# Gate and up projections of a SwiGLU layer by seven half products instead of eight, on one Trainium2 core

## The chip, the cores and the metric

The kernel runs on one core of one Trainium2 chip. The metric is the device time of one execution in microseconds (us), the median of three runs. TensorE (PE in the profile) multiplies, and loads the stationary operand of each product in a row of its own (PEld). VectorE (DVE) and ScalarE (ACT) work on tiles in SBUF and PSUM, GpSimd (POOL) adds squares, and SyncE (SP) issues the DMAs.

## The reference

One decoder layer on 512 tokens of width 1024: a SwiGLU feed-forward sub-layer, a mixer (a spatial-gating half and an attention half), cross-attention into 256 memory rows, and a second SwiGLU sub-layer. The change concerns the two feed-forward sub-layers; their hidden width is 2816.

```
def rmsnorm(t, g):
    tf = t.astype(F32)
    y = tf * lax.rsqrt(jnp.mean(tf * tf, axis=-1, keepdims=True) + NORM_EPS)
    return (y * g.astype(F32)).astype(t.dtype)
def swiglu(h, w_gate, w_up, w_down):
    return (jax.nn.silu(h @ w_gate) * (h @ w_up)) @ w_down
...
h = rmsnorm(x, ffn1_norm[l])
x = x + 0.5 * swiglu(h, ffn1_w_gate[l], ffn1_w_up[l], ffn1_w_down[l])
```

## The kernel before

Features lie on partitions and tokens on the free axis, so the residual stream is eight tiles X[0..7] of 128 x 512. Every fp32 operand is split in two rounded parts: ScalarE copies it to a high part (L103), and VectorE subtracts that from the source for a low part (L104). One fp32 product is then three matmuls (`mm3`, L127 to L129): high by high, low by high, high by low.

A feed-forward sub-layer (`ffn`) has 22 hidden tiles of 128 features, called f. For each f a gate weight tile and an up weight tile of 128 x 1024 come in, one DMA of 512 KB each, into a raw tile (`wraw`); `load_weight` splits it into `whi` and `wlo`. Each of the three names has three buffers. A weight tile takes 8 x 3 matmuls of 512 columns against the eight split tiles of x times gain (hH, hL). The row factor R (one over the root mean square) is not in these operands: `evacuate` multiplies both results by it (L243, L247), applies Silu, multiplies, and splits the product into hidH and hidL. After eleven hidden tiles a down projection adds to X: for each of eight output columns d two weight loads, 33 matmuls, and one VectorE addition (L230). So the sub-layer has two such chunks. In the last chunk of the second sub-layer the down projection runs in two halves of 256 tokens, each followed by the final normalisation and its output DMAs.

The work is written in program order; a scheduler then sets the order on each engine and in each DMA queue, and it is fixed from there on: an engine, and SP's queue of DMA issues, takes its rows one after the other, and a row that waits holds what stands behind it. The pool `hp` has 40 buffers of 128 x 512 for operands of all kinds, `pacc` and `paux` four PSUM banks each.

## Time and profile before

| what | before |
|---|---|
| median of three runs | 1129.87 us (1128.18 to 1129.97) |
| the profiled execution's own time | 1129.09 us |
| its span, first to last instruction | 1127.3 us |
| PE busy | 1110.1 us, 98% of the span |
| DVE busy | 590.9 us, 52% |
| ACT busy | 425.0 us, 38% |
| POOL busy | 74.3 us, 7% |

Busy time adds up the durations of an engine's rows, overlap counted once. Matmuls are pipelined, so a row of 390 ns does not mean that the next starts 390 ns later; what counts is the distance between starts. An idle time before a group of rows names what ended it. A window's row gives, per engine, the busy time and the number of instructions, then the granted TensorE clock (1.00 is full), the share of the DMA engines, and GB/s.

### The profile page before, as it was taken

To read this page: it belongs to the slowest core of one execution; us is meant where nothing else is said; L and a number is where in the kernel's file an instruction comes from. 1 tells how busy PE (TensorE), PEld (TensorE's weight loads), DVE (VectorE), ACT (ScalarE), POOL (GpSimd) and SP (SyncE) were. 2 spreads that over 40 slices of the span, in tenths; PEclk is the share of its full clock that TensorE was granted. 3 is DMA by queue.
4 is the path that set the end of the run, shared out by engine and by line. 5 is a ranking of instruction groups with operands and counts; after the bars stand their busy time and mean duration, and the time that the engine had idled before them with its cause. 6 is when DMAs were issued, how large, how long until landed. Compare 5 with 4: busy or idle time off the path is not lost. (4 is left out here: it accounts for less than half of the span.)

```text
span 1127.3 us, 13958 instructions
## 1 busy us (share of the span) xinstructions
PE 1110.1 (98%) x5472; PEld 934.7 (83%) x5472; DVE 590.9 (52%) x1027; ACT 425.0 (38%) x672; POOL 74.3 (7%) x98
## 2 busy tenths in 40 slices
PE   9999999999999999999989999999999999999996
PEld 7788888888888888888868988878888888888996
DVE  4544533444444447679796555455444334445542
ACT  6333312233233434568665344333332222333421
POOL 2000100000002200011121000120000000000011
PEclk9999999999999999999999999999999999999998
DMA  6322334222233423110136421222222333223511
GB/s 220 113 94 89 115 89 126 105 94 94 72 92 109 149 90 108 38 48 29 57 118 203 147 75 57 72 97 90 98 93 66 103 113 111 95 94 115 155 64 38
DMA packets 39698, 110.79 MB, mean 98 GB/s; under 512 B 4432, under 2 KB 9296, under 8 KB 39632
## 3 DMA queue, kind: packets, MB, share of 16 engines
q1 hardware_dynamic: 39632, 109.89, 30.3%
q8 instruction: 43, 0.70, 0.2%
q14 instruction: 23, 0.19, 0.1%
HBM read 107.78 MB, written 2.10 MB: 97 GB/s over the span
## 5 line engine op out<-in xcount | busy, mean ns | idle before, releaser
L103 ACT ACTIVATE whi<-wraw 128x1024 fp32r<-128x1024 f32 (+2 forms) x213 | 202.8, 953 | 513.9 <-PE acc L128 298.6
L104 DVE TENSOR_TENSOR wlo<-wraw,whi 128x1024 fp32r<-128x1024 f32 (+2 forms) x213 | 237.0, 1115 | 163.0 <-ACT whi L103 162.7
L127 PE MATMUL acc<-hH,whi 128*128 128x512 f32 x768 | 301.0, 392 | 0.6 <-ACT hH L202 0.6
L128 PE MATMUL acc<-hL,whi 128*128 128x512 f32 x768 | 299.4, 390 | 0.8 <-DVE hL L203 0.8
L129 PE MATMUL acc<-hH,wlo 128*128 128x512 f32 x768 | 299.4, 390 | 0.5 <-DVE wlo L104 0.5
L128 PEld LDWEIGHTS acc<-hL,whi 128*128 128x128 f32 x768 | 144.3, 188 | 31.5 <-DVE hL L203 1.5
L127 PEld LDWEIGHTS acc<-hH,whi 128*128 128x128 f32 x768 | 144.3, 188 | 31.4 <-ACT hH L202 1.0
L129 PEld LDWEIGHTS acc<-hH,wlo 128*128 128x128 f32 x768 | 144.3, 188 | 30.7 <-DVE wlo L104 1.0
L127 PE MATMUL acc<-hidH,whi 128*128 128x512 f32 (+1 forms) x308 | 115.6, 375 | 0.0
L129 PE MATMUL acc<-hidH,wlo 128*128 128x512 f32 (+1 forms) x308 | 115.3, 374 | 0.0
L128 PE MATMUL acc<-hidL,whi 128*128 128x512 f32 (+1 forms) x308 | 115.3, 374 | 0.0
L170 POOL TENSOR_TENSOR sq<-sq 128x512 f32<-128x512 f32 (+1 forms) x39 | 49.2, 1260 | 775.5 <-ACT sq L178 775.1
L247 DVE TENSOR_TENSOR u<-acc,R 128x512 f32<-128x512 f32 x44 | 30.4, 690 | 121.6 <-PE acc L129 121.6
L243 DVE TENSOR_TENSOR gp<-acc,R 128x512 f32<-128x512 f32 x44 | 30.4, 691 | 85.4 <-PE acc L129 81.7
L129 PEld LDWEIGHTS acc<-hidH,wlo 128*128 128x128 f32 x308 | 58.1, 189 | 10.3
L128 PEld LDWEIGHTS acc<-hidL,whi 128*128 128x128 f32 x308 | 58.1, 188 | 10.3
L127 PEld LDWEIGHTS acc<-hidH,whi 128*128 128x128 f32 x308 | 58.1, 189 | 10.2
L127 PE MATMUL acc<-whi,hH 128*128 128x512 f32 x160 | 62.5, 391 | 0.0
L129 PE MATMUL acc<-whi,hL 128*128 128x512 f32 x160 | 62.4, 390 | 0.0
L230 DVE SCALAR_TENSOR_TENSOR x<-acc,x 128x512 f32<-128x512 f32 (+1 forms) x40 | 23.3, 584 | 74.6 <-PE acc L129 74.6
L128 PE MATMUL acc<-wlo,hH 128*128 128x512 f32 x160 | 62.3, 390 | 0.0
L178 ACT ACTIVATE sq<-x 128x512 f32<-128x512 f32 (+1 forms) x48 | 26.1, 551 | 41.5 <-DVE x L230 38.9
(213 smaller groups left out, 1488.1 us busy)
## 6 DMA issues: line engine op xcount, KB each, us to landing
wraw<-up SPq DMA_DIRECT2D x44, 512.0 KB, 3.5
wraw<-gate SPq DMA_DIRECT2D x43, 512.0 KB, 3.5
wraw<-down SPq DMA_DIRECT2D x28, 384.0 KB, 3.1
wraw<-w_in SPq DMA_DIRECT2D x20, 512.0 KB, 3.5
wraw<-down SPq DMA_DIRECT2D x28, 320.0 KB, 2.9
wraw<-w_out SPq DMA_DIRECT2D x16, 256.0 KB, 2.7
wraw<-wv SPq DMA_DIRECT2D x8, 512.0 KB, 3.5
wraw<-wk SPq DMA_DIRECT2D x8, 512.0 KB, 4.2
```

Of the source, the lines that this page charges most:

```text
L103: ins = nc.scalar.activation(hi, src, AF.Copy)
L104: nc.vector.tensor_sub(lo, src, f32(hi))
L127: nc.tensor.matmul(ps, lhsT=aH, rhs=bH, start=start, stop=False)
L128: nc.tensor.matmul(ps, lhsT=aH, rhs=bL, start=False, stop=False)
L129: nc.tensor.matmul(ps, lhsT=aL, rhs=bH, start=False, stop=stop)
L170: nc.gpsimd.tensor_add(self.parts[0], self.parts[0], sq)
L178: nc.scalar.activation(sq, src, AF.Square)
L230: nc.vector.scalar_tensor_tensor(X[d][:, tok], acc, 0.5, X[d][:, tok], op0=ALU.mult, op1=ALU.add)
L243: nc.vector.tensor_mul(gp, ps[0], R)
L247: nc.vector.tensor_mul(u, ps[1], R)
```

## The change

The first two pairs of hidden tiles (f = 0 to 3) of a sub-layer stay as they were, and are now a chunk of their own. The other nine pairs go in three chunks of three pairs. For such a pair the gate product, and the up product likewise, is seen as a 2 x 2 block product: two weight tiles (rows r1 and r2 of the source), two halves of the inner dimension (k0 and k1), two halves of the tokens (LO and HI). It is formed by seven products of half the inner dimension and 256 tokens, in place of eight. The products are numbered 1 to 7 in the code; each is 4 x 3 matmuls of 256 columns. They accumulate in turns in few PSUM banks, and ScalarE copies what is needed of a stage before the next product adds to it (p1, p5, v); VectorE combines the rest.

The right operands (B11, B2, T13, T24) hold x times gain times R and differences of such tiles. `operands(k)`, called four times while f = 2 and 3 are worked on, makes them. With R in the operands, nothing is multiplied by R behind the product.

The left operands of a pair need, for each source, the two plain halves of r1 (in the raw tile `a1`, named wraw), a quarter `a22` (named wr), and four sums (ws1 to ws4). The quarter `q` (named wq) starts as r2's first half; an accumulating DMA from POOL's queue adds r2's second half; it is split as ws1; VectorE adds r1's first half; it is split as ws2; a second accumulating DMA adds r1's second half, and it is split as ws4. A third accumulating DMA adds r2's first half into the raw tile `a1` itself, which is split as ws3. So each source of a pair has three accumulating DMAs of 256 KB, and seven splits of 128 x 512 where there were two of 128 x 1024. The quarters and their splits live in `hp`, as the hidden tiles now do.

The down projections take four chunks (4, 6, 6 and 6 hidden tiles), each with one weight load per column; two columns are begun before the last two hidden tiles are there. `mem_rows`, a side computation on the memory rows, moves its two small later steps into the mixer.

```diff
-with tc.tile_pool(name="ffn", bufs=2) as fp:
+with tc.tile_pool(name="spad", bufs=1) as spad, \
+        tc.tile_pool(name="sp", bufs=1) as sp, \
+        tc.tile_pool(name="ffn", bufs=1) as fp:
+    nc.vector.memset(spad.tile([P, SHIFT], F32, name="spad")[:, 0:1], 0.0)
     R = None
-    def down_tile(d, w, hid, tok, jj, acc=None, js=range(CF)):
+    B11, B2 = ([], []), ([], [])
+    T13, T24 = ([], []), ([], [])
+    def operands(k):
+        x = []
+        for d in (k, k + KH):
+            t = hp.tile([P, S], F32, name="xg", tag="h")
+            nc.vector.scalar_tensor_tensor(t, X[d], gcol(norm.off, d), R,
+                                           op0=ALU.mult, op1=ALU.mult)
+            x.append(t)
+        a, b = x
+        t13 = hp.tile([P, S], F32, name="t13", tag="h")
+        nc.vector.tensor_sub(t13[:, LO], a[:, LO], a[:, HI])
+        nc.vector.tensor_sub(t13[:, HI], b[:, HI], a[:, HI])
+        t24 = hp.tile([P, S], F32, name="t24", tag="h")
+        nc.vector.scalar_tensor_tensor(t24[:, LO], b[:, HI], -1.0, t13[:, LO],
+                                       op0=ALU.mult, op1=ALU.subtract)
+        nc.vector.scalar_tensor_tensor(t24[:, HI], t24[:, LO], -1.0, b[:, LO],
+                                       op0=ALU.mult, op1=ALU.subtract)
+        for n, pair, src in (("b11", B11, a[:, LO]), ("b2", B2, b),
+                             ("t13", T13, t13), ("t24", T24, t24)):
+            for i, hl in enumerate("hl"):
+                pair[i].append(sp.tile([P, src.shape[-1]], F32R, name=f"{n}{hl}{k}"))
+            split(pair[0][k], pair[1][k], src)
+    def c_tile(name):
+        return fp.tile([P, S], F32, name=name, tag="c", bufs=5)
+    def half_tile(name):
+        return fp.tile([P, S // 2], F32, name=name, tag="half", bufs=5)
...
+    def down_tile(d, w, hid, tok, acc=None, js=None, cut=((0, 8),)):
+        n = len(hid[0])
         if acc is None:
             acc = acc_tile()[:, tok]
...
-    def evacuate(ps, hid):
-        gp = fp.tile([P, S], F32, name="gp", tag="gp")
-        nc.vector.tensor_mul(gp, ps[0], R)
-        s = fp.tile([P, S], F32, name="s", tag="s")
-        nc.scalar.activation(s, gp, AF.Silu)
-        u = fp.tile([P, S], F32, name="u", tag="u")
-        nc.vector.tensor_mul(u, ps[1], R)
-        nc.vector.tensor_mul(u, s, u)
-        hH = fp.tile([P, S], F32R, name="hidH", tag="hidH", bufs=12)
-        hL = fp.tile([P, S], F32R, name="hidL", tag="hidL", bufs=12)
+    def hidden(u, hid):
+        hH, hL = h_tile("hidH"), h_tile("hidL")
         split(hH, hL, u)
         hid[0].append(hH)
         hid[1].append(hL)
+    def evacuate(ps, hid):
+        gp = c_tile("gp")
+        nc.vector.tensor_mul(gp, ps[0], R)
+        nc.scalar.activation(gp, gp, AF.Silu)
+        u = c_tile("u")
+        nc.vector.tensor_mul(u, ps[1], R)
+        nc.vector.tensor_mul(u, gp, u)
+        hidden(u, hid)
+    def plain(f, src):
+        if f == 0 and src is gate and first is not None:
+            w = first()
+        else:
+            w = load_weight(src[f], [KD, P])
+        acc = acc_tile()
+        for k in range(KD):
+            mm3(acc, w, h, (slice(None), k), k, k == 0, k == KD - 1)
+        return acc
+    def quarter(name, dtype=F32R):
+        return hp.tile([P, KH, P], dtype, name=name, tag="h")
+    def strassen_weights(src, j, wa):
+        k0, k1 = slice(0, KH), slice(KH, KD)
+        r1, r2 = src[2 * j], src[2 * j + 1]
+        a1 = wp.tile([P, KD, P], F32, name="wraw", tag="wraw")
+        q, a22 = quarter("wq", F32), quarter("wr", F32)
+        nc.sync.dma_start(q, r2[:, k0])
+        nc.sync.dma_start(a1, r1)
+        last["dma"] = nc.sync.dma_start(a22, r2[:, k1])
+        nc.gpsimd.dma_start(q, r2[:, k1], accum_op=ALU.add)
+        def parts(raw, name):
+            w = quarter(name + "h"), quarter(name + "l")
+            split(w[0], w[1], raw)
+            return w
+        w = {1: wa[0], 2: wa[1]}
+        split(*w[1], a1[:, k0])
+        w[5] = parts(q, "ws1")
+        nc.vector.tensor_add(q, q, a1[:, k0])
+        w[6] = parts(q, "ws2")
+        nc.gpsimd.dma_start(a1[:, k0], r2[:, k0], accum_op=ALU.add)
+        nc.gpsimd.dma_start(q, r1[:, k1], accum_op=ALU.add)
+        split(*w[2], a1[:, k1])
+        w[7] = parts(a1[:, k0], "ws3")
+        w[3] = parts(q, "ws4")
+        w[4] = parts(a22, "wa22")
+        return w
+    def strassen(j, hid):
+        right = {1: (B11, LO), 2: (B2, LO), 3: (B2, HI), 4: (T24, HI),
+                 5: (T13, LO), 6: (T24, LO), 7: (T13, HI)}
+        wa = [[wp.tile([P, KD, P], F32R, name=n, tag=n) for n in ("whi", "wlo")]
+              for _ in range(2)]
+        W = [strassen_weights(src, j, [tuple(x[:, s * KH:(s + 1) * KH] for x in pair)
+                                       for pair in wa])
+             for s, src in enumerate((gate, up))]
+        z = [acc_tile()[:, HI] for _ in range(2)]
+        b1, b5 = [None] * 2, [None] * 2
...
+        def product(ps, i, s, start):
+            b, tok = right[i]
+            wH, wL = W[s][i]
+            for k in range(KH):
+                bH, bL = b[0][k][:, tok], b[1][k][:, tok]
+                for n, (x, y) in enumerate(((wH, bH), (wH, bL), (wL, bH))):
+                    nc.tensor.matmul(ps, lhsT=x[:, k], rhs=y,
+                                     start=start and k == 0 and n == 0,
+                                     stop=k == KH - 1 and n == 2,
+                                     skip_group_check=True)
+        def copied(ps, name):
+            t = half_tile(name)
+            nc.scalar.activation(t, ps, AF.Copy)
+            return t
+        for s in range(2):
+            product(z[s], 1, s, True)
+            p1[s] = copied(z[s], "p1")
+        for s in range(2):
+            b5[s] = aux_tile()[:, HI]
+            product(b5[s], 5, s, True)
+            p5[s] = copied(b5[s], "p5")
+        for s in range(2):
+            product(z[s], 6, s, False)
+            v[s] = copied(z[s], "v")
+        for s in range(2):
+            b1[s] = aux_tile()[:, HI]
+            product(b1[s], 2, s, True)
+            nc.vector.tensor_add(c1[s][:, LO], b1[s], p1[s])
+        for s in range(2):
+            product(z[s], 7, s, False)
+            nc.vector.scalar_tensor_tensor(c2[s][:, HI], z[s], -1.0, p5[s],
+                                           op0=ALU.mult, op1=ALU.subtract)
+        for s in range(2):
+            product(b5[s], 3, s, False)
+            nc.vector.tensor_add(c1[s][:, HI], b5[s], v[s])
+        for s in range(2):
+            product(z[s], 4, s, False)
+        nc.scalar.activation(c1[0], c1[0], AF.Silu)
+        nc.scalar.activation(c2[0][:, HI], c2[0][:, HI], AF.Silu)
+        nc.scalar.activation(c2[0][:, LO], z[0], AF.Silu, scale=-1.0)
+        nc.vector.tensor_mul(c1[1], c1[0], c1[1])
+        hidden(c1[1], hid)
+        nc.vector.tensor_mul(c2[1][:, HI], c2[0][:, HI], c2[1][:, HI])
+        nc.vector.scalar_tensor_tensor(c2[1][:, LO], z[1], -1.0, c2[0][:, LO],
+                                       op0=ALU.mult, op1=ALU.mult)
+        hidden(c2[1], hid)
+    chunks = ((0, PLAIN),) + tuple((j, j + 3) for j in range(PLAIN, NF // 2, 3))
+    for c, (j0, j1) in enumerate(chunks):
         hid = ([], [])
+        for j in range(j0, j1):
+            if j >= PLAIN:
+                strassen(j, hid)
+                continue
+            for f in (2 * j, 2 * j + 1):
+                ps = [plain(f, gate)]
+                if R is not None and f > 1:
+                    operands(2 * f - 4)
+                if f == 1 and R is None:
+                    R = factor()
+                ps.append(plain(f, up))
+                pending.append(ps)
+                if first is None and f == 0:
+                    R = factor()
+                if R is not None:
+                    while pending:
+                        evacuate(pending.pop(0), hid)
+                if f > 1:
+                    operands(2 * f - 3)
+        f0, n = 2 * j0, 2 * (j1 - j0)
+        if c < len(chunks) - 1 or nxt is not None:
+            early = {}
+            for d in range(2):
+                w = [load_weight(down[d, :, f0:f0 + n, :], [n, P])]
+                early[d] = w, down_tile(d, w, hid, slice(0, S), None, range(n - 2))
+            for d in range(KD):
+                if d in early:
+                    w, acc = early[d]
+                    down_tile(d, w, hid, slice(0, S), acc, range(n - 2, n))
+                    w = [load_weight(down[d, :, f0:f0 + n, :], [n, P])]
+                    down_tile(d, w, hid, slice(0, S))
+                if c == len(chunks) - 1:
                     nxt.add(d)
-                elif between is not None:
-                    between(d)
+                    if between is not None:
+                        between(d)
             continue
...
-        thirds = ((0, 4), (4, 8), (8, CF))
+        cut = ((0, 4), (4, 6))
+        def weights(d):
+            if d not in kept:
+                raw = wp.tile([P, n, P], F32, name="wraw3", tag="wraw")
+                nc.sync.dma_start(raw, down[d, :, f0:f0 + n, :])
+                a, b, m = (h_tile("wk").rearrange("p (j m) -> p j m", m=P)
+                           for _ in range(3))
+                kept[d] = [(a, b), (m[:, 0:2], m[:, 2:4])]
+                for pair, (i0, i1) in zip(kept[d], cut):
+                    split(*pair, raw[:, i0:i1])
+            return kept[d]
...
             if t0 == 0:
-                for d in range(2):
-                    w, cut = weights(d, True)
-                    early[d] = down_tile(d, w, hid, tok, cut, None, range(CF - 1))
+                for d in range(3):
+                    early[d] = down_tile(d, weights(d), hid, tok, None, range(n - 2),
+                                         cut)
...
     z_block(norm, 0, gelu_to(U), lambda: col.append(norm.stats.column(D)))
+    mem_rows(2)
     z_block(norm, 1, gelu_to(V))
+    mem_rows(4)
...
 with tc.issue_after(last["dma"].ins):
     if d == 0:
         cs.append(rotary_tables(small))
-    mem_rows(d)
+        mem_rows(0)
...
-return np.ascontiguousarray(w.reshape(NCHUNK, CF, P, KD, P).transpose(0, 3, 2, 1, 4))
+return np.ascontiguousarray(w.reshape(NF, P, KD, P).transpose(2, 1, 0, 3))
```

What the scheduler makes of it is shown at three places of the second chunk of three pairs in the first sub-layer. The first place is SP's queue. Tiles are named with their numbers: 1836 and 1870 are the gate and up raw tiles of the chunk's first pair, 2118 and 2152 of its second, 2400 and 2434 of its third; wq and wr are the quarters of the tile numbered one or two lower. Before:

```order
L116 DMA wraw_687<-up1 128x1024
L116 DMA wraw_729<-gate1 128x1024
L116 DMA wraw_760<-up1 128x1024
L116 DMA wraw_802<-gate1 128x1024
L116 DMA wraw_833<-up1 128x1024
```

And with the change:

```order
L327 DMA wraw_2118<-gate1 128x1024
L327 DMA wraw_2152<-up1 128x1024
L326 DMA wq_1871<-up1 128x512
L328 DMA wr_1872<-up1 128x512
L327 DMA wraw_2400<-gate1 128x1024
L326 DMA wq_2119<-gate1 128x512
L328 DMA wr_2120<-gate1 128x512
L327 DMA wraw_2434<-up1 128x1024
L326 DMA wq_2153<-up1 128x512
L328 DMA wr_2154<-up1 128x512
L118 DMA wraw_2678<-down1 128x768
L118 DMA wraw_2697<-down1 128x768
```

The quarter of each source now stands behind the raw tile of a source three further on, which takes the buffer of the raw tile one source back. The second place is VectorE in the second pair, where whole-tile splits stood between evacuations before:

```order
L243 TENSOR_TENSOR gp_791<-acc_735,R_309 128x512
L104 TENSOR_TENSOR wlo_835<-wraw_833,whi_834 128x1024
L247 TENSOR_TENSOR u_795<-acc_766,R_309 128x512
L248 TENSOR_TENSOR u_795<-s_793,u_795 128x512
L104 TENSOR_TENSOR wlo_877<-wraw_875,whi_876 128x1024
L104 TENSOR_TENSOR hidL_799<-u_795,hidH_798 128x512
```

And with the change, the gate source (2118, 2119) and then the up source (2152, 2153):

```order
L106 TENSOR_TENSOR ws1l_2128<-wq_2119,ws1h_2127 128x512
L338 TENSOR_TENSOR wq_2119<-wq_2119,wraw_2118 128x512
L106 TENSOR_TENSOR ws2l_2133<-wq_2119,ws2h_2132 128x512
L106 TENSOR_TENSOR ws3l_2141<-wraw_2118,ws3h_2140 128x512
L106 TENSOR_TENSOR ws4l_2145<-wq_2119,ws4h_2144 128x512
L106 TENSOR_TENSOR wa22l_2149<-wr_2120,wa22h_2148 128x512
L106 TENSOR_TENSOR wlo_2397<-wraw_2434,whi_2396 128x512
L106 TENSOR_TENSOR wlo_2399<-wraw_2434,whi_2398 128x512
L106 TENSOR_TENSOR ws1l_2162<-wq_2153,ws1h_2161 128x512
L338 TENSOR_TENSOR wq_2153<-wq_2153,wraw_2152 128x512
L106 TENSOR_TENSOR ws2l_2167<-wq_2153,ws2h_2166 128x512
```

ws3 of the gate source is the last reader of raw tile 2118, whose buffer raw tile 2434 takes; the up source's ws1 stands behind. The third place is TensorE behind the second pair's gate products, with the change (before, each product was 24 matmuls of 512 columns into one accumulator, one weight tile after the other):

```order
L370 MATMUL acc_2469<-b11h3_602,whi_2396 128x256
L370 MATMUL acc_2469<-b11l3_603,whi_2396 128x256
L370 MATMUL acc_2469<-b11h3_602,wlo_2397 128x256
L370 MATMUL aux_2235<-t13h0_419,ws1h_2161 128x256
L370 MATMUL aux_2235<-t13l0_420,ws1h_2161 128x256
```

Product 1 of the third pair's up source (acc_2469) now stands ahead of product 5 of the second pair's up source (aux_2235), which in the code comes first.

More of the change, by code (lines that the diff above doesn't have):

```diff
@@ L41 @@
 SB = 6
+PLAIN = 2
 LINE = 512
 FILL = 56
+SHIFT = 112
 G_FFN1, G_MIX, G_CROSS, G_MEM, G_FFN2, G_FIN, G_OA, G_OB, G_BS = (
@@ L226, in down_tile @@
                                 mm3(acc, (wH, wL), hid, (slice(None), j - j0),
-                                    (j, slice(None), tok), j == 0, j == CF - 1)
-                    if CF - 1 not in js:
+                                    (j, slice(None), tok), j == 0, j == n - 1)
+                    if js is not None and n - 1 not in js:
                         return acc
@@ L286, in ffn @@
                                 nxt.add(d)
-                            elif between is not None:
-                                between(d)
+                                if between is not None:
+                                    between(d)
                         continue
-                    thirds = ((0, 4), (4, 8), (8, CF))
+                    cut = ((0, 4), (4, 6))
                     kept = {}
-                    def weights(d, keep):
-                        if d in kept:
-                            return kept[d], thirds
-                        if not keep:
-                            return [load_weight(down[c, d, :, j0:j1, :], [j1 - j0, P])
-                                    for j0, j1 in halves], halves
-                        kept[d] = []
-                        for j0, j1 in thirds:
-                            raw = wp.tile([P, j1 - j0, P], F32, name="wraw3", tag="wraw")
-                            nc.sync.dma_start(raw, down[c, d, :, j0:j1, :])
-                            pair = tuple(h_tile("wk")[:, :(j1 - j0) * P]
-                                         .rearrange("p (j m) -> p j m", m=P) for _ in range(2))
-                            split(*pair, raw)
-                            kept[d].append(pair)
-                        return kept[d], thirds
```

50 lines of the change are left out of this document (12 added, 38 removed).

## The prediction

> **What bounds the kernel now.** I read the page's busy times first, then its chain of waits, then busy time by window.
>
> ```profile
> PE 1110.1 (98%) x5472; PEld 934.7 (83%) x5472; DVE 590.9 (52%) x1027; ACT 425.0 (38%) x672; POOL 74.3 (7%) x98
> PE acc L128 11%; PE acc L129 11%; PE acc L127 11%; DVE o L330 0%; PE aux L153 0%; PE aux L186 0%; DVE rcolt L141 0%; DVE rcolt L142 0%; DVE rcoly L143 0%; DVE x L230 0%; ACT sq L178 0%; DVEq L889 0%; DVE dg L151 0%; DVE rcoly L136 0%; DVE rcolv L134 0%
> 32.00:273.00 241.00, 240.98 (x1063) 199.05 (x1062) 112.51 (x153) 72.31 (x94) 5.25 (x4) 1.00 0.31 99
> 1050.00:1107.00 57.00, 57.00 (x474) 56.87 (x473) 22.11 (x50) 14.26 (x26) 7.87 (x10) 1.00 0.28 86
> ```
>
> TensorE has no gap: the chain is matmuls, and in the feed-forward windows (columns: length, then PE, PEld, DVE, ACT, POOL, clock, DMA share, GB/s) it is busy throughout at full clock. The first window holds 512-column matmuls and gives 241.0 / 1063 = 0.2267 us from start to start; the second, the token-halved down projection, holds 256-column ones and gives 57.0 / 474 = 0.1203. VectorE has half its time free, DMA two thirds. So less matmul time shows in the span, as long as operands arrive in time.
>
> **What the change removes.** A pair cost 4 x 24 x 0.2267 = 21.8 us; now it is 2 x 7 x 12 = 168 matmuls at 0.1203 = 20.2. The saving is 1.55 us, not an eighth (2.7), since a 256-column matmul takes 53% of a 512-column one. Eighteen pairs give 27.9. In the last down projection five of eleven hidden tiles leave the halved form: 120 x (2 x 0.1203 - 0.2267) = 1.7. The tail behind the last matmul does not change.
>
> The Trainium skill ("TensorE: Matmul & The Clock Gate", section Back-to-back issue gap) has 262 and 518 cycles, 109 and 216 ns at 2.4 GHz. By these a pair would save 20.7 - 18.3 = 2.4 us; the windows' spacing decides, and gives 1.55.
>
> **What it adds on VectorE and ScalarE.**
>
> ```profile
> L104 DVE TENSOR_TENSOR wlo<-wraw,whi 128x512 fp32r<-128x512 f32 x18 | 12.1, 686 | 1.3 <-ACT whi L103 1.2
> L103 ACT ACTIVATE whi<-wraw 128x512 fp32r<-128x512 f32 x18 | 11.3, 628 | 5.5 <-PE acc L128 3.0 <-PE acc L129 1.9 <-DMA wraw<-gate 0.3
> L104 DVE TENSOR_TENSOR kL<-acc,kH 128x256 fp32r<-128x256 f32 x8 | 3.3, 418 | 0.0
> L466 DVE SCALAR_TENSOR_TENSOR vL<-acc,rcoly,vH 128x512 fp32r<-128x512 f32 x4 | 3.0, 749 | 1.7 <-ACT vH L465 1.7
> L666 DVE SCALAR_TENSOR_TENSOR mraw<-mraw,gains,R 128x256 f32<-128x256 f32 x8 | 3.7, 479 | 0.0
> L247 DVE TENSOR_TENSOR u<-acc,R 128x512 f32<-128x512 f32 x44 | 30.4, 690 | 121.6 <-PE acc L129 121.6
> L248 DVE TENSOR_TENSOR u<-s,u 128x512 f32<-128x512 f32 x44 | 30.8, 703 | 3.8 <-ACT s L245 0.5
> L230 DVE SCALAR_TENSOR_TENSOR x<-acc,x 128x512 f32<-128x512 f32 x24 | 16.6, 692 | 44.9 <-PE acc L129 44.9
> ```
>
> Per pair VectorE has 14 splits and 2 additions of 128 x 512 (0.69), eight half-width combinations (0.42 to 0.48), one full product and two hidden splits: 11.0 + 3.6 + 2.1 = 17 us. ScalarE has 14 splits (0.63), six half copies, Silu and two hidden splits: 14 us. Both lie under the 20.2 of TensorE, so neither is the bound there.
>
> `operands` is denser. One call is two products of 0.75, two half differences of 0.42, two of 0.48, and splits of 0.42 + 3 x 0.69: 5.8 us, four times 23.2. From the moment R is ready to the split of the down weights of column 3, VectorE has these, four evacuations (three products and a split, 4 x 2.8 = 11.1), two whole-tile splits of 1.25, four of 0.69 and three additions to X: 41.7 us. TensorE gets there in 21.8 + 3 x 12 x 0.2267 = 30.0. In the timeline R is used first at 33.45; the third tile's gate product is evacuated from 39.97, so TensorE began it about 24 x 0.2267 earlier, 34.4 with the hand-off. By durations TensorE waits 10.8. But VectorE's rows overlap: these start 0.61 apart and last 0.69, which takes an eighth off and leaves 6. I take 8 per sub-layer, 16 in all; the bounds are 6 and 11.
>
> ```profile
> 33.45 0.69 DVE L243 TENSOR_TENSOR gp<-acc,R 128x512 f32<-128x512 f32 x1 [1.85 <-ACT R L157]
> 34.06 0.68 DVE L247 TENSOR_TENSOR u<-acc,R 128x512 f32<-128x512 f32 x1
> 37.05 1.22 DVE L104 TENSOR_TENSOR wlo<-wraw,whi 128x1024 fp32r<-128x1024 f32 x1
> 39.97 0.69 DVE L243 TENSOR_TENSOR gp<-acc,R 128x512 f32<-128x512 f32 x1 [0.49 <-PE acc L129]
> ```
>
> **What it adds as waits.** This is the term that decides. A source's weights now pass through a series: quarter loaded, accumulating DMA, ws1 split, addition, accumulating DMA into the raw tile, ws3 split. Only then is the raw tile's buffer free. SP's order puts the next source's quarter load behind the raw load that needs this very buffer, so one source's series cannot begin before the last one's is over; and the down loads, SP's next rows, wait in the same line. Its prices:
>
> ```profile
> L116 SPq DMA_DIRECT2D wraw<-gate x45: 327/328/432, 1.6 to 1014.7; - x45
> wraw<-up SPq DMA_DIRECT2D x44, 512.0 KB, 3.5
> wraw<-down SPq DMA_DIRECT2D x28, 384.0 KB, 3.1
> wraw<-w_out SPq DMA_DIRECT2D x16, 256.0 KB, 2.7
> const<-const SPq DMA_DIRECT2D x1, 388.0 KB, 6.7
> gains<-gains SPq DMA_DIRECT2D x1, 32.0 KB, 1.7
> L103 ACT ACTIVATE whi<-wraw 128x768 fp32r<-128x768 f32 x28 | 23.7, 847 | 71.4 <-PE acc L128 61.7 <-issue 7.7 <-DMA wraw<-down 1.7
> L104 DVE TENSOR_TENSOR wlo<-wraw,whi 128x768 fp32r<-128x768 f32 x28 | 27.5, 981 | 2.6 <-ACT whi L103 2.5
> 1115.31 0.42 DVE L230 SCALAR_TENSOR_TENSOR x<-acc,x 128x256 f32<-128x256 f32 x1 [3.54 <-PE acc L129]
> 1115.82 0.42 ACT L178 ACTIVATE sq<-x 128x256 f32<-128x256 f32 x1 [3.54 <-DVE x L230]
> ```
>
> An issue holds SP 0.33. A quarter lands behind a 512 KB load, so I take 3.5. A hand-off between engines is 1115.82 - 1115.73 = 0.1, seven times. Let A be an accumulating DMA from its release to its data. One link is two issues 0.7 + landing 3.5 + A + (0.63 + 0.69 + 0.69 =) 2.0 + A + (0.63 + 0.69 =) 1.3 + hand-offs 0.7 = 8.2 + 2A.
>
> The trace has no accumulating DMA. I expect it no quicker than a plain load of its 256 KB, 2.7, and the slowest load, 6.7, is the other end. It reads its target too, so twice the bytes: nearest is the 512 KB row, 3.5, and with another issue A = 3.8. A link is then 15.8 us, while a source is 10.1 us of TensorE work.
>
> The Trainium skill ("DMA: Bandwidth & Descriptors", section Anatomy of one DMA) fits 2.0 us plus bytes over 436 GB/s for a plain DMA of POOL's queue, 2.6 us here, most of it the receipt of the write; by that the sum would come out near the lower end below.
>
> Now a chunk of three pairs, from the end of one down projection to the end of the next. The first pair's gate tile was prepared during that down projection, its ws3 split about 1 us before the end. Then come four links in a row: up of the first pair, gate and up of the second, gate of the third. The last one has a detour of 5.3: SP's two down loads stand ahead of its quarter, and the second of them waits for the split of the first (0.33 + 3.1 + 0.85 + 0.98). Then the third pair's up: two issues, landing, accumulate, ws1's high part and three hand-offs, 5.1 + A. Only now can its product 5 start, with 108 half matmuls left in the pair (13.0) and 120 full ones in the down projection (27.2). Together -1 + 4 x (8.2 + 2A) + 5.3 + 5.1 + A + 13.0 + 27.2 = 82.4 + 9A = 116.6 us. TensorE's own work is 3 x 20.2 + 144 x 0.2267 = 93.3, and the same work took 3 x 21.8 + 32.6 = 97.9 before. So TensorE waits 23 us in a chunk, and the chunk is 18.7 longer: six chunks, 112.2. (The 27.9 saved is in this difference.)
>
> Waits cost clock too:
>
> ```profile
> 576.00:580.00 4.00, 0.83 (x3) 0.42 (x4) 4.00 (x7) 1.31 (x3) 1.27 (x1) 1.00 0.00 0
> 582.00:584.00 2.00, 2.00 (x6) 1.53 (x5) 2.00 (x5) 1.79 (x3) 0.40 (x1) 0.50 0.31 125
> 580.68 0.55 PE L129 MATMUL acc<-yH,wlo 128*128 128x512 f32 x1
> 584.01 0.47 PE L127 MATMUL acc<-yH,whi 128*128 128x512 f32 x1
> ```
>
> After 4 us with 0.83 busy, the clock granted is 0.50 for 3.3 us (the matmuls are longer from 580.68 to 584.01). The wait ahead of the last product 5 is of that size, and it lies on the path; half of it, 1.7, is lost per chunk, 10.2 in all.
>
> The sum: 112.2 + 16 + 10.2 - 1.7 = +136.7 us. On the profiled execution's span of 1127.3 this is 1264.0, on its own time of 1129.09 it is 1265.8; the median is 0.8 above that, so **1267 us**.
>
> What costs nothing: p1, v and p5 copies and the combinations (ScalarE and VectorE have room in waits of 23 us), 16 more additions to X per sub-layer (0.69 each, under the next column's 18 matmuls of 4.1 us), the moved `mem_rows` steps (two matmuls and a few short rows), and 27 MB more DMA traffic at 30% load. Without cover the additions would be 22 us.
>
> **Rivals.**
>
> First, the series does not bind, because an accumulating DMA is far quicker than any load. A chunk breaks even where 82.4 + 9A equals 97.9 less the other terms' 4.1, at A = 1.3; below 1.2 it is TensorE's alone, and 1129.9 - 27.9 - 1.7 + 16 = 1116. For it: TensorE's rate is proven by the window of 256 columns. Against: no load in the page lands under 2 us except a 32 KB one at 1.7.
>
> Second, A is short but not that short: 2.0, as if the fixed part of a load were all. Then a chunk is 100.4, and the sum is 15.0 + 24.5 = +39.5, 1169. Speaking for it is the 0.8 us between 256 and 512 KB (2.7 and 3.5), which leaves 1.9 as the part without bytes.
>
> Third, A is long, as in the row of 6.7: a chunk is 142.7, 1423. Each us of A is worth 54 us, so this price is the whole width of the range.
>
> That 256-column matmuls would be held back by weight loads (PEld busy 56.87 of 57.00 us in the second window) is excluded by the spacing of 0.1203 in that same window.
>
> **How the numbers follow.** The series binds with A between 2.0 and 5.3 (1169 to 1348): 0.78. Above that 0.08. Below 2.0 and still slower 0.04. A measurement of this kernel tells 0.2% (2.3 us) from no change; within that 0.02. The first rival, or that I misread the order in which the loads wait, 0.08 and faster. So slower 0.90, same 0.02, faster 0.08. The range goes from 1165 to 1348 and leaves out 0.08 above and about as much below.
>
> **What would show it.** In the changed profile: SP's waits on the ws3 splits at every raw load; TensorE idle ahead of ws1 and ws4 products, some 20 us a chunk, most in its second and third pair; clock below 1.00 right behind; POOL's accumulating DMAs landing near 3.8 us. The product rows should keep 0.12 us from start to start. I am wrong if the accumulating DMAs land under 1.5 us, if TensorE stays at 98% busy, or if VectorE, with 17 us a pair, is the one that TensorE waits for while the quarters lie ready.

## The result and the profile after

The changed kernel takes 1336.44 us (1332.89 to 1339.63) against 1129.41 for the kernel before: a ratio of 1.1828, 95% interval [1.1814, 1.1842]. That is 207 us slower; 1267 was forecast, with a range up to 1348. The profiled execution has a span of 1337.8 us, 210.5 more than before. First the page's busy times and its chain of waits, by engine and by line, then TensorE's two longest waits (in all, times, longest).

```profile
PE 1165.4 (87%) x6648; PEld 1019.5 (76%) x6648; DVE 744.2 (56%) x1409; ACT 544.7 (41%) x1008; POOL 169.3 (13%) x206
PE 15%; DMA 11%; issue 5%; DVE 3%; ACT 1%; POOL 0%; SPq 0%; POOLq 0%; DVEq 0%; ACTq 0%
DMA wq<-up 4%; PE acc L131 3%; PE acc L130 3%; PE acc L129 3%; PE aux L370 3%; DMA wraw<-gate 3%; PE acc L370 2%; DMA wq<-gate 1%; DMA wraw<-up 1%; DMA wr<-up 1%; DVE ws3l L106 1%; ACT ws3h L105 1%; POOL wq L329 0%; ACT ws1h L105 0%; DVE xg L244 0%
```

```profile
PE aux L370 <- ACT ws1h L105: 88.3, 26, 5.4
PE aux L370 <- ACT ws4h L105: 46.7, 12, 4.7
```

TensorE is no longer alone in the chain: beside its 15% of the span the quarters' and raw tiles' transfers stand in it with 11%. TensorE waits 135 us for ws1 and ws4, 22.5 a chunk in the mean of six (23 were forecast). The timeline shows one source's series from beginning to end: from the ws3 split of the source before to its own.

```profile
105.88 0.69 DVE L106 TENSOR_TENSOR ws3l<-wraw,ws3h 128x512 fp32r<-128x512 f32 x1
106.59 0.33 SPq L327 DMA_DIRECT2D wraw<-gate  x1
106.97 0.42 SPq L326 DMA_DIRECT2D wq<-gate  x1
...
111.50 0.86 POOL L329 DMA_DIRECT2D wq<-gate  x1 [9.33 <-DMA wq<-gate]
116.04 0.62 ACT L105 ACTIVATE ws1h<-wq 128x512 fp32r<-128x512 f32 x1
117.42 0.69 DVE L338 TENSOR_TENSOR wq<-wq,wraw 128x512 f32<-128x512 f32 x1
118.53 0.88 POOL L340 DMA_DIRECT2D wraw<-gate  x1 [6.17 <-DVE wq L338]
122.81 0.63 ACT L105 ACTIVATE ws3h<-wraw 128x512 fp32r<-128x512 f32 x1 [3.53 <-DMA wraw<-gate]
123.47 0.69 DVE L106 TENSOR_TENSOR ws3l<-wraw,ws3h 128x512 fp32r<-128x512 f32 x1 [3.96 <-ACT ws3h L105]
124.19 0.33 SPq L327 DMA_DIRECT2D wraw<-up  x1
124.56 0.43 SPq L326 DMA_DIRECT2D wq<-up  x1
125.22 0.58 PE L370 MATMUL aux<-b2h,ws4h 128*128 128x256 f32 x1 [4.24 <-ACT ws4h L105]
```

The raw load is issued 0.02 us after ws3's low split ends (105.88 + 0.69 = 106.57), and the quarter's load right behind it, which had nothing else to wait for (ahead of all 36 quarter loads together SP's waits add up to 3.3 us). From 106.57 to 124.16 the link takes 17.6 us: 0.4 to the quarter's issue, 4.5 until GpSimd can add to it, 4.5 for that accumulating DMA, 2.1 for split and addition, 4.7 for the one into the raw tile, 1.4 for ws3. Meanwhile TensorE waits and, after waits, runs at a lower clock. The issues of these DMAs (KB each, median us to landing):

```profile
wq<-gate POOLq DMA_DIRECT2D x36, 256.0 KB, 4.3
wraw<-gate POOLq DMA_DIRECT2D x18, 256.0 KB, 4.2
wq<-gate SPq DMA_DIRECT2D x18, 256.0 KB, 3.7
```

### The profile page after: what moved, and what is told of

Its sections match the earlier page's. It is cut to its first block, busy times and chain, and to the rows that moved or that the text cites. A ratio compares the mean times of both kernels' runs of the same rounds, so it can differ in the third digit from the quotient of the medians.

```text
span 1337.8 us, 17404 instructions
## 1 busy us (share of the span) xinstructions
PE 1165.4 (87%) x6648; PEld 1019.5 (76%) x6648; DVE 744.2 (56%) x1409; ACT 544.7 (41%) x1008; POOL 169.3 (13%) x206
## 5 line engine op out<-in xcount | busy, mean ns | idle before, releaser
L105 ACT ACTIVATE whi<-wraw 128x512 fp32r<-128x512 f32 (+2 forms) x213 | 168.4, 801 | 236.4 <-PE acc L130 113.3
L106 DVE TENSOR_TENSOR wlo<-wraw,whi 128x512 fp32r<-128x512 f32 (+2 forms) x213 | 194.5, 924 | 117.2 <-ACT whi L105 116.0
L370 PE MATMUL aux<-t13h,ws1h 128*128 128x256 f32 x144 | 52.9, 368 | 88.5 <-ACT ws1h L105 88.3
L129 PE MATMUL acc<-hidH,whi 128*128 128x512 f32 x304 | 118.8, 399 | 9.3 <-ACT hidH L105 5.1
L130 PE MATMUL acc<-hidL,whi 128*128 128x512 f32 x304 | 120.9, 398 | 0.2
L131 PE MATMUL acc<-hidH,wlo 128*128 128x512 f32 x304 | 119.3, 396 | 1.6 <-DVE wlo L106 1.6
L370 PE MATMUL aux<-b2h,ws4h 128*128 128x256 f32 x144 | 48.3, 335 | 46.7 <-ACT ws4h L105 46.7
L129 PE MATMUL acc<-hH,whi 128*128 128x512 f32 x192 | 76.6, 399 | 0.0
L130 PE MATMUL acc<-hL,whi 128*128 128x512 f32 x192 | 75.0, 391 | 0.8 <-DVE hL L205 0.8
L131 PE MATMUL acc<-hH,wlo 128*128 128x512 f32 x192 | 75.0, 391 | 0.5 <-DVE wlo L106 0.5
```

Of the source, the lines that this page charges most:

```text
L105: ins = nc.scalar.activation(hi, src, AF.Copy)
L106: nc.vector.tensor_sub(lo, src, f32(hi))
L129: nc.tensor.matmul(ps, lhsT=aH, rhs=bH, start=start, stop=False)
L130: nc.tensor.matmul(ps, lhsT=aH, rhs=bL, start=False, stop=False)
L131: nc.tensor.matmul(ps, lhsT=aL, rhs=bH, start=False, stop=stop)
L370: nc.tensor.matmul(ps, lhsT=x[:, k], rhs=y, start=start and k == 0 and n == 0, stop=k == KH - 1 and n == 2, skip_group_check=True)
```

## Experiments

Theories. **Series**: each source's preparation waits for the last one's, through SP's order of loads. **Queue**: three accumulating DMAs per source on one queue bind whatever SP does. **VectorE**: its work and order bind. Later, **clock**: TensorE's halved clock is on the path. Runs with one time only have no interval.

### Quarters with buffers of their own

```diff
-        hp = ctx.enter_context(tc.tile_pool(name="hp", bufs=40))
+        hp = ctx.enter_context(tc.tile_pool(name="hp", bufs=37))
-    q, a22 = quarter("wq", F32), quarter("wr", F32)
+    q, a22 = fp.tile([P, KH, P], F32, name="wq", tag="q", bufs=3), quarter("wr", F32)
```

> The quarters q get three buffers of their own (and the common pool 37 in place of 40), so SP's order has a quarter's load behind the ws4 split of the source three before it, no longer behind the raw load that waits for the ws3 split of the source just before. All 108 accumulating DMAs stay. Series theory: the next source's quarter is loaded and summed while this one is worked on, what is left from source to source is ws1 split, addition, one accumulating DMA and ws3 split with the splits behind it, some 9.5 us against TensorE's 10.1; the time falls to 1120 to 1165 us, and TensorE's waits for ws1 (88 us) fall below 20. Queue theory (three accumulating DMAs of 4.5 us in a row per source, 13.5 us, bind whatever SP does): six chunks of six sources at 13.5 and a down projection, 1290 to 1340. VectorE theory (its order and its 17 us a pair bind): 1300 to 1340.

Measured: 1214.22 us (1203.96 to 1216.33), ratio to before 1.0721 [1.0669, 1.0772]. With every accumulating DMA kept, 122 of the 207 us are gone, so SP's order is the larger cause, and the queue theory and the VectorE theory fall. Its time lies above the series theory's range, though. TensorE's waits:

```profile
PE aux L370 <- ACT ws4h L105: 46.6, 17, 4.2
PE aux L370 <- ACT ws1h L105: 8.0, 7, 2.2
```

Those for ws1 fell below 20 us as expected, those for ws4 stayed. The timeline shows what is late now:

```profile
107.51 0.63 ACT L105 ACTIVATE hidH<-u 128x512 fp32r<-128x512 f32 x1 [0.88 <-DVE u L409]
108.05 0.62 ACT L105 ACTIVATE ws1h<-wq 128x512 fp32r<-128x512 f32 x1
110.60 0.86 POOL L340 DMA_DIRECT2D wraw<-gate  x1 [5.62 <-DVE wq L338]
112.02 0.86 POOL L341 DMA_DIRECT2D wq<-gate  x1 [0.55 <-DVE ws2l L106]
117.45 0.63 ACT L105 ACTIVATE ws4h<-wq 128x512 fp32r<-128x512 f32 x1 [1.96 <-DMA wq<-gate]
118.13 0.58 PE L370 MATMUL aux<-b2h,ws4h 128*128 128x256 f32 x1 [3.92 <-ACT ws4h L105]
118.51 0.61 ACT L105 ACTIVATE ws1h<-wq 128x512 fp32r<-128x512 f32 x1
```

The next pair's quarter is there, but its ws1 split stands behind the last hidden tile of the pair before on ScalarE (hidH, 107.51), and behind the split the DMAs begin, 5.4 us from the last one's issue to ws4's split. The up source's ws1 split in turn stands behind ws4's. From one ws3 split to the next, the up sources of this run take 8.8 to 10.9 us, the gate sources of second and third pairs 19.1 to 24.4. A second series, on ScalarE's order, had been hidden by the first. That is read from the timeline; no run changed ScalarE's order by itself.

### One accumulating DMA on the path, and one beside it

```diff
# on the path (ws1)
-    nc.gpsimd.dma_start(q, r2[:, k1], accum_op=ALU.add)
+    nc.vector.tensor_add(q, q, a22)
# beside it (ws4), in another kernel
-    nc.gpsimd.dma_start(q, r1[:, k1], accum_op=ALU.add)
+    nc.vector.tensor_add(q, q, a1[:, k1])
```

> The first accumulating DMA of each source (4.5 us from release to the ws1 split) becomes an addition of the two loaded quarters on VectorE, 0.69, which waits for the second quarter, 0.5 later. SP's order is as it was. Series theory: a link falls from 17.5 to 14.2, and there are five of them in a chunk, so six chunks lose 6 x 5 x 3.3 = 99 us: 1235, and not below 1200. Queue theory: two thirds of the queue's work, 9 us a source, below TensorE's 10.1: 1120 to 1160. VectorE theory: 1.4 us a pair more work, slower than 1336.

> The second accumulating DMA on the quarter (it makes ws4, and nothing of SP's waits for it) becomes an addition of the raw tile's second half on VectorE. SP's order is as it was. Series theory: the link keeps its 17.5 us; TensorE's waits for ws4 (47 us) go, but the time they took is waited for ws1 in the next source, so 1310 to 1340. Queue theory: as for the first accumulating DMA, 1120 to 1160.

Measured: 1271.18 and 1336.29 us. The same kind of DMA, taken away in the same number, is worth 65 us where SP's next load hangs on it and nothing where none does. That again is the series and not the queue. The first gave 65 and not 99 because of ScalarE's order once more. Its timeline, with the quarter issued at 216.18:

```profile
216.18 0.42 SPq L326 DMA_DIRECT2D wq<-gate  x1
225.71 0.63 ACT L105 ACTIVATE hidH<-u 128x512 fp32r<-128x512 f32 x1 [1.20 <-DVE u L409]
229.88 0.63 ACT L105 ACTIVATE ws1h<-wq 128x512 fp32r<-128x512 f32 x1 [1.09 <-DVE wq L329]
230.56 0.39 PE L370 MATMUL aux<-t13h,ws1h 128*128 128x256 f32 x1 [1.18 <-ACT ws1h L105]
```

For this gate source of a second pair, 13.7 us pass from the load to the split, and the hidden tiles of the first pair lie between. The link of the up source behind it is 14.4 us, as expected. In the six chunks the second pair's gate link takes 18.8 to 21.8, where it took 17.6 to 20.7 in the changed kernel: it grew by 1.4 in the mean where 3.3 less was expected, and six times 4.7 is 28 of the 34 us that are missing.

### A fourth raw buffer

```diff
-    a1 = wp.tile([P, KD, P], F32, name="wraw", tag="wraw")
+    a1 = wp.tile([P, KD, P], F32, name="wraw", tag="wraw", bufs=4)   # and the other raw tiles; hp 38
```

> Four raw buffers in place of three (and 38 in the common pool for 40). SP's order then has one more raw or down load ahead of each quarter, and the load just ahead of it waits for the ws3 split of the source just before, as now. Series theory: the buffers' number is not what binds but the order of the loads, so 1320 to 1350. Rival (raw buffers are short, and one more lets two sources overlap): 1130 to 1180.

Measured: 1333.86 us. Buffers were not short; the order was wrong. One more only lets SP take one more load ahead of the same wait.

### Sums without accumulating DMAs, then without either series

```diff
+    s3 = quarter("w3", F32)
+    nc.vector.tensor_add(s3, a1[:, k0], q)            # for ws3
-    nc.gpsimd.dma_start(q, r2[:, k1], accum_op=ALU.add)
+    nc.vector.tensor_add(q, q, a22)
-    nc.gpsimd.dma_start(a1[:, k0], r2[:, k0], accum_op=ALU.add)
-    nc.gpsimd.dma_start(q, r1[:, k1], accum_op=ALU.add)
+    nc.vector.tensor_add(q, q, a1[:, k1])
...
-    w[7] = parts(a1[:, k0], "ws3")
+    w[7] = parts(s3, "ws3")
```

> No accumulating DMA is left: ws3's, ws1's and ws4's sums are additions on VectorE (the first half of the raw tile plus the quarter into a tile of its own, then the second quarter and the raw tile's second half onto the quarter), 0.69 each and 4.2 us a pair more on VectorE. Quarters stay in the common pool, so SP's order still has each quarter behind a raw load that waits for the source just before, now for the last of its additions. Series theory: a link is 0.7 + 5.0 for both quarters + 1.4 + 2.1 + 1.4 + 0.7 and hand-offs = 11.6 us, still above the 10.1 of TensorE; 5 x 5.9 less in a chunk gives 1160, and where the next pair's first ws1 split stands behind this pair's hidden tiles on ScalarE, as the runs with own quarters and with the first sum on VectorE showed, up to 1200. If the accumulating DMAs were all of it: 1105 to 1130. VectorE theory (now 21 us a pair): 1250 or more.

Measured: 1209.56 us, 10 above the upper figure. Without a single accumulating DMA, but with the quarters still in line behind the raw loads, the kernel is as slow as with all of them and the quarters free (1214). For the next two, r2 also comes whole, into three buffers of its own:

```diff
-        hp = ctx.enter_context(tc.tile_pool(name="hp", bufs=40))
+        hp = ctx.enter_context(tc.tile_pool(name="hp", bufs=34))
-    q, a22 = quarter("wq", F32), quarter("wr", F32)
-    nc.sync.dma_start(q, r2[:, k0])
-    last["dma"] = nc.sync.dma_start(a22, r2[:, k1])
+    b1 = fp.tile([P, KD, P], F32, name="wb", tag="wb", bufs=3)
+    q, a22 = b1[:, k0], b1[:, k1]
+    last["dma"] = nc.sync.dma_start(b1, r2)
# the second kernel: nc.gpsimd instead of nc.vector for s3 and for q + a22
```

> Both causes taken away: r2 comes whole, as one 512 KB load into a tile with three buffers of its own (the common pool has 34), so no quarter waits for the source just before, and all sums are on VectorE as additions, without an accumulating DMA. Series theory: no series is left, TensorE's waits fall below 25 us, and the time is TensorE's: 1127 less 29.6 of matmuls plus 6 for the operands' backlog that the changed kernel shows gives 1105 to 1130. VectorE theory (21 us a pair by durations, against TensorE's 20.2): 1140 to 1180.

> As the one before, but the sums for ws3 and ws1 are on GpSimd (about 1.5 us each, 6 us a pair), so VectorE has 18.4 us a pair. Series theory: as before, 1105 to 1130, the same within 10 us. VectorE theory: 20 to 40 us faster than with all sums on VectorE. Rival: GpSimd's additions stand in the way of VectorE's, and it is slower than with VectorE alone.

Measured: 1147.14 us, ratio 1.0161 [1.0144, 1.0178], and 1139.87, 1.0101 [1.0074, 1.0127]. Both changes together give back 189 to 197 of 207 us. Neither reached 1105 to 1130; the first lies where the VectorE theory put it. But GpSimd's help was worth 7 us and not the 20 to 40 of that theory, so neither theory fits both runs. With all sums on VectorE, TensorE's longest wait is this one:

```profile
PE aux L373 <- ACT ws1h L105: 20.2, 20, 2.6
```

### Plain products first

```diff
# product 2 (plain halves only) ahead of product 5 (needs the ws1 split)
     for s in range(2):
         product(z[s], 1, s, True)
         p1[s] = copied(z[s], "p1")
+    for s in range(2):
+        b1[s] = aux_tile()[:, HI]
+        product(b1[s], 2, s, True)
+        nc.vector.tensor_add(c1[s][:, LO], b1[s], p1[s])
     for s in range(2):
         b5[s] = aux_tile()[:, HI]
         product(b5[s], 5, s, True)
...
-    for s in range(2):
-        b1[s] = aux_tile()[:, HI]
-        product(b1[s], 2, s, True)
-        nc.vector.tensor_add(c1[s][:, LO], b1[s], p1[s])
```

> The kernel with whole r2 tiles and all sums on VectorE, and product 2, which needs only plain halves, ahead of product 5, which needs the ws1 split. In the run before TensorE waited 1.2 us for ws1 in twenty pairs' openings, 20 us in all, since the ws1 split stands behind the last hidden tile of the pair before on ScalarE. Theory (that short hand-over is what was left of the waits): 5.8 us of plain products cover it, and 12 to 20 us go: 1127 to 1135. Rival (VectorE, 21 us of rows a pair against 20.2, is the bound, and the wait reappears at another product): 1142 to 1150, as before.

> The same order of products with ws3's and ws1's sums on GpSimd. TensorE's waits there were 6 us for ws1, 6 for copies p, 3 for ws2. Theory: 6 to 12 us go, 1126 to 1134, about the time of the kernel before. Rival: the later products then meet VectorE's backlog, 1138 to 1145.

Measured: 1137.19 us, ratio 1.0059 [1.0046, 1.0072], and 1130.42, ratio 1.0004 [0.9994, 1.0014]. Ten us each: half of the first's 20 us of waits, and in the second a time that can't be told from before. The first lies between its two ranges: the wait for the hand-over was the cause of those 10, but 7 us more than with GpSimd's help remain, so that VectorE's load has a share too. Windows of the second, from the first use of R to the last addition of the first feed-forward sub-layer:

```profile
33.50:66.00 32.50, 31.25 (x136) 24.91 (x134) 31.67 (x60) 17.47 (x31) 0.00 (x0) 1.00 0.15 41
66.00:84.00 18.00, 15.83 (x74) 12.44 (x72) 12.46 (x18) 4.17 (x8) 8.11 (x6) 1.00 0.37 117
84.00:181.00 97.00, 92.57 (x640) 84.81 (x641) 73.85 (x110) 46.86 (x90) 21.26 (x13) 1.00 0.34 102
181.00:278.00 97.00, 95.66 (x674) 88.29 (x673) 73.03 (x108) 43.48 (x84) 18.19 (x13) 1.00 0.33 100
278.00:372.00 94.00, 92.03 (x632) 84.33 (x631) 73.01 (x114) 52.59 (x99) 25.81 (x19) 1.00 0.36 108
```

The kernel before, the same stretch:

```profile
33.50:372.80 339.30, 339.28 (x1498) 280.82 (x1498) 156.26 (x207) 105.36 (x139) 16.50 (x11) 1.00 0.31 98
```

TensorE's busy time in the sub-layer is 327.3 against 339.3, so the seven products do save 12 us (13.9 forecast, 9 x 1.55). But it now idles 11.2 us there, where it idled 0.02 before: 10.9 in waits that the timeline names, 6.9 of them for VectorE and 4.0 for ScalarE. What the arithmetic saves, the hand-overs take.

Two further edits tried to win those back.

```diff
# first: half differences of operands on GpSimd
-        nc.vector.tensor_sub(t13[:, LO], a[:, LO], a[:, HI])
-        nc.vector.tensor_sub(t13[:, HI], b[:, HI], a[:, HI])
+        nc.gpsimd.tensor_sub(t13[:, LO], a[:, LO], a[:, HI])
+        nc.gpsimd.tensor_sub(t13[:, HI], b[:, HI], a[:, HI])
# second: ws1's sum on VectorE into a tile of its own
-    nc.gpsimd.tensor_add(q, q, a22)
+    w1 = quarter("w1", F32)
+    nc.vector.tensor_add(w1, q, a22)
+    q = w1
```

> As the one before, and the two half differences of each call of operands on GpSimd: 8 rows of 0.42 us less on VectorE in a sub-layer, while it is behind (TensorE waited 3.3 us for it around the first down projection, and its clock was halved for 3.4 us behind that). Backlog theory: 3 to 6 us faster than the same kernel without it. Rival: GpSimd's rows are slower (some 0.8 us) and VectorE waits for them, so nothing is won.

> As the kernel with whole r2 tiles, product 2 ahead of product 5 and ws3's and ws1's sums on GpSimd, but ws1's sum is on VectorE, into a tile of its own, so that it does not stand behind GpSimd's 1.5 us for ws3's; GpSimd has 3 us a pair, VectorE 19.8. TensorE waited 4.5 us for ws2, 2.8 for copies v and 5.6 for plain low parts in that run. Theory (GpSimd's two sums in a row are what made ws2 late): 4 to 8 us go, 1122 to 1127, faster than the kernel before. Rival (VectorE at 19.8 us a pair has no room): 1130 to 1138, as with all sums on VectorE.

Measured: 1133.36 us, ratio to before 1.0026 [1.0017, 1.0036], and 1129.92, ratio 0.9994 [0.9985, 1.0003]. The first is 3 us slower than without it, where its theory had 3 to 6 us faster. The second is the same, so GpSimd's two sums in a row were not what cost 4 to 8 us. No version of this change that was run beats the kernel before.

### Filling TensorE's waits

```diff
+    for i in range(24):
+        nc.tensor.matmul(b5[s], lhsT=W[s][1][0][:, i % KH], rhs=B11[0][i % KH],
+                         start=True, stop=True, skip_group_check=True)
     product(b5[s], 5, s, True)
```

> The changed kernel with 24 half-width matmuls more, whose result is overwritten, ahead of each product 5 (36 times, 2.9 us each at full clock, 104 us in all), where TensorE waited for ws1 (88 us in 26 waits). Nothing else is moved. Series theory: TensorE's own time and clock lie off the path but for the last pair of a chunk; the extra work is hidden in the waits and the clock is halved less often, so 1315 to 1350, and the 201 us at half clock become fewer without the time following. Clock theory (the 85 us by which TensorE's rows are longer than at full clock are on the path): 1250 to 1290. If TensorE's own work were on the path: 1400 or more.

Measured: 1355.89 us, 6 above the series theory's range. Its page's busy times:

```profile
PE 1233.4 (91%) x7512; PEld 1095.8 (81%) x7512; DVE 743.7 (55%) x1409; ACT 545.5 (40%) x1008; POOL 169.2 (12%) x206
```

TensorE's 104 us of added work lengthen the span by 16 (1354.1 against 1337.8). The mean granted clock rises from 0.925 to 0.955; if the clock is either full or half, that is 122 us at half clock in place of 201, and the time doesn't follow. So the clock theory, with all of its 85 us on the path, is not borne out. A smaller part isn't excluded, since this run adds work as well as clock. That 16 us do show fits the path through ScalarE's order: hidden tiles wait for TensorE, and the next pair's ws1 split waits for them.

## Why the prediction was right, and where its sum was off

**The sign and the mechanism.** The series through SP's order was the decisive term, and it is shown: cutting it alone gives 122 of the 207 us, and each piece taken out of it or from beside it moves the time accordingly. Its signs came too: TensorE idle ahead of ws1 and ws4, a lower clock behind the waits, accumulating DMAs at 4.1 to 4.3 us (near 3.8 was expected).

Its sum was 136.7 us, and 210.5 were measured. The time lies within the range, but the range was drawn by A alone, and that it held is in part luck: with A at 4.6, the mean of the two in the series above, the prediction's own formula gives 136.7 + 54 x 0.8 = 180 us, about 1310. The other 30 us came from steps for which the range had no room. The terms, one by one:

**A chunk** was forecast at 116.6 + 1.7 = 118.3 us. From the last addition of one down projection to that of the next it took 128.9 in these two rows; five such chunks took 128.9 to 133.9, 131.9 in the mean.

```profile
217.96 0.68 DVE L280 SCALAR_TENSOR_TENSOR x<-acc,x 128x512 f32<-128x512 f32 x1
...
346.87 0.68 DVE L280 SCALAR_TENSOR_TENSOR x<-acc,x 128x512 f32<-128x512 f32 x1
```

The window from the last ws1 split in it to its end:

```profile
303.20:346.87 43.67, 43.66 (x238) 38.64 (x239) 25.65 (x41) 16.45 (x28) 4.37 (x5) 0.93 0.47 118
```

The excess of 13.6 us, taken for the sixth chunk too, is 82 us, a little more than the whole miss of 74. It has four parts, here in the chunk between these rows (10.6 in excess). First, the link was sized at 15.8 and is 16.7 to 17.8 where nothing disturbs it: A was taken as 3.8 and is 4.5 and 4.7 in the series above, and the quarter can be added to 4.5 us after its issue (3.7 in the median to its landing alone), where 3.5 was taken. Second, one of the four links, the second pair's gate, took 19.5: its ws1 split stands behind the first pair's hidden tiles, and a weight split that follows them, on ScalarE. The prediction followed SP's queue row by row, but judged ScalarE by its load alone ("Both lie under the 20.2 of TensorE, so neither is the bound there"); this step was wrong in kind, not in size. The four links with the detour (the last quarter was issued 5.1 later than without it, forecast 5.3) took 77.3 where 68.5 was forecast. Third, the way from the last link to the split of ws1 was 9.7 for 8.9. Fourth, **the clock**: 43.7 us from the last ws1 split to the chunk's end, for 40.2 of work, at a granted 0.93. So some 3 us are lost on the path where 1.7 was taken.

**Half clock.** The first row below has the wait, the second the clock behind it:

```profile
220.00:226.00 6.00, 2.83 (x25) 2.63 (x23) 2.08 (x3) 2.72 (x7) 0.86 (x1) 1.00 0.42 96
226.00:230.00 4.00, 3.54 (x19) 3.55 (x20) 2.08 (x3) 1.25 (x3) 1.24 (x2) 0.64 0.00 0
```

TensorE's busy time grew by 55 us though its work shrank by some 30. Read as a cost, that would be 85 us of clock; but the windows above put only some 3 us a chunk, 18 in six, on the path. The rest fell in time that was waited through anyway, and the run with filled waits agrees.

**The backlog of operands** was put at 8 us per sub-layer. The rows at which TensorE waited around the first down projection add up to 3.3:

```profile
59.49 0.47 PE L129 MATMUL acc<-hidH,whi 128*128 128x512 f32 x1 [0.83 <-DVE gp L299]
60.60 0.50 PE L131 MATMUL acc<-hidH,wlo 128*128 128x512 f32 x1 [0.40 <-DVE wlo L106]
68.19 0.47 PE L129 MATMUL acc<-hidH,whi 128*128 128x512 f32 x1 [1.62 <-DVE x L280]
69.89 0.66 PE L131 MATMUL acc<-hidH,wlo 128*128 128x512 f32 x1 [0.40 <-DVE wlo L106]
```

```profile
66.00:85.00 19.00, 16.98 (x71) 13.25 (x70) 13.90 (x23) 5.80 (x11) 2.77 (x3) 0.91 0.59 148
```

With a clock of 0.91 in the 19 us around and behind them, 1.7 more, it is 5 us. The term was over-sized by 3 and lies below its lower bound of 6; the mechanism is there. The sum now closes: 136.7 + 82 for the chunks - 6 for two backlogs is 213, and 210.5 were measured.

**The product's spacing.** The first and the last of 43 half-width rows in a row stand 4.95 us apart, 0.118 from start to start, close to the 0.1203 taken.

```profile
104.50 0.28 PE L370 MATMUL acc<-t24l,ws2h 128*128 128x256 f32 x1
...
109.45 0.28 PE L370 MATMUL aux<-b2h,ws4h 128*128 128x256 f32 x1
```

The Trainium skill ("TensorE: Matmul & The Clock Gate", section Back-to-back issue gap) has 262 cycles, 109 ns at 2.4 GHz, for a matmul without its weight load; the 118 ns here lie between that and the 120 of the kernel before. For a plain DMA of this size on POOL's queue the Trainium skill's fit gives an estimate of 2.6 us ("DMA: Bandwidth & Descriptors", section Anatomy of one DMA); the accumulating ones take longer, 4.1 to 4.3.

**The rivals.** A of 1.3 or less (1116) and of 2.0 (1169) fall with the DMA's 4.1 to 4.3 us; so does 6.7. The first rival's arithmetic was nearly right for what it assumed: with the waits out of the way the sub-layer's matmul time falls by 12 us. Its time, 1116, was not reached by any run, since hand-overs of 11 us a sub-layer remained.

## What to carry to other kernels

When a step gets a series of dependent transfers, follow every in-order queue on it, the engines' as well as the DMA queue's: a load whose buffer is free can still stand behind one whose buffer is not, and a buffer more doesn't help where the order is at fault. Take one series out and look for the next at once; here ScalarE's order stood behind SP's. And weigh the saving against the hand-overs first: seven products for eight saved 12 us of 339, and keeping TensorE without a gap was worth as much.

## What the runs showed of the hardware

GpSimd's additions slow VectorE's, where the two run side by side. Rows of VectorE grouped by line, in the kernel with whole r2 tiles and all sums on VectorE:

```profile
L106 DVE TENSOR_TENSOR ws4l<-wb,ws4h 128x512 fp32r<-128x512 f32 x36 | 24.8, 688 | 5.2 <-ACT ws4h L105 4.2
L280 DVE SCALAR_TENSOR_TENSOR x<-acc,x 128x512 f32<-128x512 f32 x56 | 37.6, 686 | 24.0 <-PE acc L131 24.0
```

The same groups with two sums per source on GpSimd:

```profile
L106 DVE TENSOR_TENSOR ws4l<-wb,ws4h 128x512 fp32r<-128x512 f32 x36 | 33.2, 921 | 7.0 <-ACT ws4h L105 6.3
L280 DVE SCALAR_TENSOR_TENSOR x<-acc,x 128x512 f32<-128x512 f32 x56 | 38.0, 684 | 29.7 <-PE acc L131 29.6
```

The same split takes 921 ns in place of 688 in the mean, while the addition that reads one operand from PSUM keeps its 0.68. The mean hides two kinds of rows: by the timeline 27 of the 36 splits have no addition of GpSimd's beside them and take 0.69, and the nine that overlap one take 1.44 to 1.78. One of these, with the addition beside it:

```profile
190.20 1.81 POOL L331 TENSOR_TENSOR w<-wraw,wb 128x512 f32<-128x512 f32 x1 [5.47 <-DMA wraw<-up]
190.79 1.77 DVE L106 TENSOR_TENSOR ws4l<-wb,ws4h 128x512 fp32r<-128x512 f32 x1
```

A split that starts first is not held: one at 181.19 us began 0.11 before an addition of GpSimd's and took 0.68, the next, at 181.79, began within that addition and took 1.79. Seven of the PSUM additions began within one of GpSimd's and lay beside it for most of their length, and took 0.68. So moving 72 rows away left VectorE's busy time where it was (806.3 and 807.8 us). The Trainium skill ("SBUF — State Buffer", section Who interferes with whom) says that a VectorE instruction with two SBUF inputs contends with a GpSimd instruction that reads SBUF, and one with at most one, outside the 2-port modes, does not; this trace agrees on both. That the 3 us lost with the half differences on GpSimd have this cause was not shown.

An accumulating DMA of 256 KB on POOL's queue lands 4.1 to 4.3 us after its issue, 0.87 of which GpSimd is held, where a plain load of the same size on SP's took 2.7 for w_out and 3.7 to 4.0 for a quarter behind a 512 KB load. How much of that is the addition and how much the queue, no run here separates.
